# A two-layer encoder in fp32 on one core: 54 background columns with a scratch pool of their own, the rows' second column group for all tokens, and attention's first head with two depth pairs plain

## The chip, the cores and the metric

The kernel runs on one core of a Trainium2 chip. The metric is the device time of one execution in microseconds. Five engines matter: PE (matmul; its weight loads are listed as PEld), DVE (vector), ACT (scalar), POOL and SP. POOL and SP do little but issue DMAs here. All matrix products are fp32, made as three products of a high and a low half.

## The reference, cut to what matters

Batch 1, 512 tokens, width 2048, two layers, each with its own normalisation, conditioning, mixer and gate:

```python
mod = silu(c) @ ada_w                       # shifts, scales, gates: 128 columns of 128 numbers
# layer A: mLSTM, 8 heads, keys 256, values 512 wide
h = rmsnorm(x, g) * (1 + scale) + shift
qk = silu(causal_conv(h @ w_in[:, :4096]))  # 4 taps
v, o, z, gates = the rest of h @ w_in
ht = rmsnorm(mlstm(q, k, v, gates))         # per head: scores, decay, num / max(|den|, exp(-m))
x = x + gate * rmsnorm((sigmoid(o) * ht * silu(z)) @ a_w_out)
# one shared key and value from x
k, v = modulate(rmsnorm(x), ...) @ kv_w
# layer B: 16 heads, band of chunks, learned relative bias
q, z = modulate(rmsnorm(x), ...) @ b_w_in
x = x + gate * rmsnorm((attention(q, k, v) * silu(z)) @ b_w_out)
```

## The kernel before

Tokens stand along the free axis (512 columns), features on partitions. Weights come from one DRAM stream in **pieces** of 512 KB (128 x 1024 floats), in the order that `stream()` writes out, by SP's queue into three `raw` buffers. `split` makes two halves of each piece: the high one by a cast on ACT, the low one by a subtraction on DVE (both at line L243; tile `wh`). PE then runs `mm3` (L311): high·high, high·low, low·high. A piece serves 24 matmuls of 512 columns where all tokens go at once (2 depth tiles x 4 blocks, or 8 depth tiles of one block, x 3), and 12 where only one **token pair** of two goes (`PAIRS`).

Part of the products use half sums: `proj_s` and `proj_v` make seven products of 256 columns where eight would stand (banks D, C, A, B; sums of inputs by `three_sums`, sums of weights at L282 to L284, tiles `ws` and `wsh`). A product that does not use them is called **plain**. `proj_s` takes `f` depth pairs by half sums and the others plain; `pair_pieces` says which pairs share a piece.

The stages in time: an opening (0 to about 205 us) with the input's normalisation and the first products; mLSTM heads 0 and 1, plain (to about 430); head 2 (`HALF`) with a ramp, heads 3 to 7 by half sums (to about 1425); the product with `a_w_out`, here called **rows** (1425 to 1754), in four column groups `g` of 512: first depth half of all, then second depth half with group 0 for all tokens and groups 1 to 3 once per token pair; then residual, normalisation and transposes (`residual`, `turned`, `key_inputs`), values and keys (to 2076); 16 attention heads (to 2450); the last product and output.

**The background.** `mod` has one column of 128 numbers per 1 MB tile of `ada_w`: the tile `ada` is loaded and summed by one long DVE operation (L552, 2.3 us). Those needed early are made in the opening; 57 are made during heads 0 and 1 by calls of `background(n)`: sum up to n loaded tiles, then load until three are in flight, by POOL's queue. `SHIFTS` says how many of the 57 are shift columns of the second layer; the other shift columns (`whole`, 19) are loaded by SP and summed among the rows (`whole_steps`, `whole_sum`).

**Scratch.** Pool `tp`, tag `t`, has three buffers of 128 x 512. Convolution sums (`cv`), copies (`cu`, `g32`), squares (`sq`), gates (`sz`) and the two rows of each head (`row_out`: the norm's parts, written to DRAM by POOL's queue and read back into `f` by `factor`) all take turns in it.

**The order of the work.** The framework places each engine's instructions in a fixed order at build time from their data, their buffers and priorities; `tc.high_priority` moves an operation ahead, `pin` keeps operations in the program's order, `behind` puts one after another without a wait. What an engine waits for later does not change its order.

In attention, `queries(h, steps)` runs one head's `proj_s` over `b_w_in`; `steps` are calls between its pieces. The inputs `h2` and their sums `h2s` are made by `input_sums`, up to the first head's pieces.

## Time and profile before

| what | value |
|---|---|
| runs shown: median (lowest to highest) | 2637.78 us (2635.75 to 2638.52), 3 runs |
| the profiled execution | 2635.22 us |
| its span, mean granted clock of TensorE | 2633.4 us, 0.997 |
| PE, DVE, ACT busy | 2574.4, 2335.1, 1428.7 us |
| weight pieces of 512 KB by SP | 506 |
| DMA, HBM traffic over the span | 510.62 MB moved, 195 GB/s |

A row of waits reads: engine, operation and line, what it waited for, then the total in us, the count and the longest. A row of the timeline reads: start, length, engine, line, operation, tile written and tiles read, shapes, how many in a row, and in brackets the idle time before it with what ended it. A row of the windows gives the stretch, the busy time and number of instructions of PE, PEld, DVE, ACT and POOL, the granted clock of PE (1.00 is full), the busy share of the DMA engines and GB/s. "ps_..." are PSUM banks, "wh" and "wsh" split weights and weight sums.

### The profile page before, as it was taken

What the parts mean: (1) busy time and instruction counts of PE and PEld (TensorE: products, weight loads), DVE (VectorE), ACT (ScalarE), POOL (GpSimd) and SP (SyncE); (2) the same over time, 40 slices, a digit from 0 to 9 for tenths busy, and PEclk for the clock granted to TensorE, in tenths of its full rate; (3) what the DMA queues carried; (4) which work ended last, traced back from release to release, by engine and by line L of the source; (5) the groups of instructions that cost most, each with busy time, mean ns of one, the idle gap of its engine ahead of it and who ended that gap; (6) DMA issues with size and microseconds to landing.
All of it is one profiled execution on the core that took longest, in us unless ns stands there. A gap on an engine that the chain in (4) does not pass through costs nothing.

```text
span 2633.4 us, 45758 instructions
## 1 busy us (share of the span) xinstructions
PE 2574.4 (98%) x17994; PEld 2407.5 (91%) x17994; DVE 2335.1 (89%) x3812; ACT 1428.7 (54%) x2106; POOL 59.8 (2%) x118
## 2 busy tenths in 40 slices
PE   8999999999999999999999999999999999999998
PEld 6887787899999999999999898788999899999887
DVE  8978988999989999899998886977997999999767
ACT  4344533466555665556655453578543766776523
POOL 0000111000000000000000000000000000000000
PEclk9999999999999999999999999999999999999999
DMA  9876787533333333333336548988654544444787
GB/s 364 313 265 251 272 329 290 192 108 114 124 102 129 115 111 125 105 125 118 110 130 237 195 150 327 301 259 302 226 179 146 171 130 138 138 130 132 254 299 251
DMA packets 155315, 510.62 MB, mean 194 GB/s; under 512 B 17893, under 2 KB 31749, under 8 KB 140633
## 3 DMA queue, kind: packets, MB, share of 16 engines
q1 hardware_dynamic: 144346, 443.89, 49.6%
q0 software_dynamic: 10752, 63.79, 6.6%
q8 instruction: 141, 2.31, 0.4%
q14 instruction: 76, 0.62, 0.1%
HBM read 473.96 MB, written 38.90 MB: 195 GB/s over the span
## 4 chain that ended last, share of the span: by engine, by line
PE 56%; DVE 25%; DMA 8%; issue 7%; ACT 3%; POOL 0%; SPq 0%; DVEq 0%; ACTq 0%; POOLq 0%
DVE wh L243 6%; PE ps_y L311 5%; PE ps_azo L311 4%; PE ps_czo L311 4%; PE ps_dzo L311 4%; DVE ada L552 3%; PE ps_y_True L311 3%; PE ps_dz L311 3%; PE ps_cz L311 3%; PE ps_y_False L311 3%; PE ps_az L311 3%; DMA wr<-in_wst 3%; DVE wsh L243 2%; PE ps_bzo L311 2%; DVE cv L797 2%
## 5 line engine op out<-in xcount | busy, mean ns | idle before, releaser
L243 ACT CAST wh<-wr 128x1024 fp32r<-128x1024 f32 (+1 forms) x536 | 553.3, 1034 | 473.3 <-DVE wr L283 102.0
L243 DVE TENSOR_TENSOR wh<-wr,wh 128x1024 fp32r<-128x1024 f32 (+1 forms) x536 | 643.3, 1203 | 127.2 <-ACT wh L243 126.3
L243 ACT CAST wsh<-ws 128x768 fp32r<-128x768 f32 (+1 forms) x296 | 241.8, 817 | 298.4 <-PE ps_az L311 67.1
L243 DVE TENSOR_TENSOR wsh<-ws,wsh 128x768 fp32r<-128x768 f32 (+1 forms) x296 | 276.8, 935 | 45.7 <-ACT wsh L243 44.5
L552 DVE CUSTOM_DVE_ANT_0 ada<-ada,scB,cl 128x2048 f32<-128x2048 f32 (+1 forms) x89 | 205.8, 2322 | 11.3 <-DMA ada<-in_adaT 11.2
L282 DVE TENSOR_TENSOR ws<-wr 128x512 f32<-128x512 f32 (+1 forms) x296 | 198.5, 673 | 5.3 <-DMA wr<-in_wst 5.0
L311 PE MATMUL ps_y_False<-wh,y 128*128 128x512 f32 x768 | 168.6, 380 | 2.3 <-DVE wh L243 2.2
L311 PE MATMUL ps_y<-wh,y 128*128 128x512 f32 x768 | 168.6, 380 | 0.1
L311 PEld LDWEIGHTS ps_y_False<-wh,y 128*128 128x128 f32 x768 | 144.3, 189 | 24.4 <-DVE wh L243 4.2
L311 PEld LDWEIGHTS ps_y<-wh,y 128*128 128x128 f32 x768 | 144.3, 189 | 20.8 <-DVE wh L243 0.5
L311 PE MATMUL ps_kv<-wh,hkv 128*128 128x512 f32 x576 | 127.3, 381 | 1.6 <-DVE wh L243 1.5
L311 PE MATMUL ps_v<-wh,h 128*128 128x512 f32 x576 | 127.3, 380 | 0.0
L311 PEld LDWEIGHTS ps_kv<-wh,hkv 128*128 128x128 f32 x576 | 108.0, 189 | 18.5 <-DVE wh L243 3.3
L284 DVE TENSOR_TENSOR ws<-wr 128x256 f32<-128x256 f32 (+1 forms) x296 | 122.1, 414 | 3.1
L283 DVE TENSOR_TENSOR wr<-ws,wr 128x256 f32<-128x256 f32 (+1 forms) x296 | 121.8, 413 | 2.4
L311 PEld LDWEIGHTS ps_v<-wh,h 128*128 128x128 f32 x576 | 108.3, 189 | 15.8 <-issue 0.9
L311 PE MATMUL ps_l<-h,wh 128*128 128x512 f32 x480 | 107.7, 380 | 2.1 <-DVE wh L243 2.1
L311 PEld LDWEIGHTS ps_l<-h,wh 128*128 128x128 f32 x480 | 90.3, 189 | 16.5 <-DVE wh L243 3.3
L311 PE MATMUL ps_azo<-h,wh 128*128 128x256 f32 (+1 forms) x606 | 92.9, 285 | 0.0
L311 PE MATMUL ps_y_True<-wh,y 128*128 128x512 f32 x384 | 83.3, 379 | 0.0
L311 PEld LDWEIGHTS ps_y_True<-wh,y 128*128 128x128 f32 x384 | 72.5, 189 | 10.2
L311 PEld LDWEIGHTS ps_azo<-h,wh 128*128 128x128 f32 x606 | 79.2, 192 | 1.1
(431 smaller groups left out, 5825.2 us busy)
## 6 DMA issues: line engine op xcount, KB each, us to landing
wr<-in_wst SPq DMA_DIRECT2D x506, 512.0 KB, 3.7
ada<-in_adaT POOLq DMA_DIRECT2D x57, 1024.0 KB, 7.1
ada<-in_adaT SPq DMA_DIRECT2D x49, 1024.0 KB, 7.0
ada<-in_adaT SPq DMA_DIRECT2D x36, 512.0 KB, 6.5
wr<-in_wst SPq DMA_DIRECT2D x26, 384.0 KB, 6.2
xt<-nsc SPq DMA_DIRECT2D x32, 256.0 KB, 3.8
yr<-ysc SPq DMA_DIRECT2D x28, 256.0 KB, 5.4
ysc<-zo SPq DMA_DIRECT2D x24, 256.0 KB, 3.9
```

The lines of the kernel that those rows point to most:

```text
L243: ins = nc.scalar.copy(hi, src), nc.vector.tensor_tensor(lo, src, hi.bitcast(F32), op=ALU.subtract)
L282: nc.vector.tensor_tensor(t[:, : 2 * w], r[:, w : 3 * w], r[:, : 2 * w], op=ALU.subtract)
L283: nc.vector.tensor_tensor(r[:, w : 2 * w], t[:, w : 2 * w], r[:, :w], op=ALU.add)
L284: nc.vector.tensor_tensor(t[:, 2 * w :], r[:, 3 * w :], r[:, w : 2 * w], op=ALU.subtract)
L311: product[0] = nc.tensor.matmul(ps, a, b, start=start, stop=stop)
L552: pin(nc.vector.tensor_tensor_reduce(c, c, (sc or scB)[:, j * w : (j + 1) * w], 1.0, mod[:, i : i + 1] if j else col(CB + i), ALU.mult, AL ...
L797: nc.vector.scalar_tensor_tensor(acc[:, d:], ps[:, : S - d], col(CW + 32 * (3 - d) + ch), acc[:, d:], op0=ALU.mult, op1=ALU.add)
```

## The change

It has four parts. Lines of the changed kernel stand some rows further down: L311 is L316 there, L243 is L248, L552 is L560.

1. **Background.** `SHIFTS` goes from 9 to 6: 54 columns in the front, and 22 instead of 19 among the rows. Four tiles may be in flight, in a ring over two pools' buffers and one of a new pool. The calls begin six steps earlier in the opening, and from then on are spread: one sum between the two pieces of a block (`mid`) and smaller counts elsewhere.
2. **A pool `t0`** from the end of the opening, with three buffers for convolution sums, two for copies, two for rows and one for an ada tile; it serves heads 0 to 2 (rows: 0 and 1), which leave `tp`. Head 0's mask sum stands after its v product, and the loads of the relative bias move from all heads to heads 3 to 7.
3. **Rows.** Group 1 runs for all tokens (8 pieces) with seven column loads between its pieces; only groups 2 and 3 run per token pair. This takes 8 pieces out of the stream. The calls of three groups of the second pair stand in two; some key inputs and transposes move on into the values; the last token group's `xr` goes into the key sums' buffers.
4. **Attention's first head.** `ATT_FIRST` is 6: pairs 6 and 7 are plain in head 0. Its first two pieces are half-sum pieces of two pairs each, the others one half-sum pair and one plain pair (`late`); a plain product into bank B is done as two halves of 256. The sums of pairs 6 and 7 (`plain_sums`) are made at steps 2 and 3 of head 0.

In counts: PE has 12 more matmuls of 512 columns and 18 fewer of 256; SP issues 8 transfers of 512 KB fewer and 3 of 1 MB more, POOL 3 of 1 MB fewer; ACT and DVE have 8 splits of a piece fewer each.

```diff
@@ -30 +30 @@
-SHIFTS = 9
+SHIFTS = 6
@@ -48,0 +49 @@
+ATT_FIRST = 6
@@ -81 +82 @@
-def pair_pieces(f, merged=False):
+def pair_pieces(f, merged=False, late=False):
@@ -87,0 +89,3 @@
+    if late:
+        out = [([[a]], [b]) for a, b in zip(sk[f - n :], nk)]
+        return [([sk[i : i + 2]], []) for i in range(0, f - n, 2)] + out
@@ -119,2 +123,2 @@
-    def tile_s(mat, c1, c2, f, merged=False):
-        for sk, nk in pair_pieces(f, merged):
+    def tile_s(mat, c1, c2, f, merged=False, late=False):
+        for sk, nk in pair_pieces(f, merged, late):
@@ -155,0 +160 @@
+    tile_b("a_w_out", 512, KT)
@@ -157 +162 @@
-        for g in range(1, 4):
+        for g in range(2, 4):
@@ -167 +172 @@
-        tile_s("b_w_in", h * P, D + h * P, ATT_PAIRS, True)
+        tile_s("b_w_in", h * P, D + h * P, ATT_PAIRS if h else ATT_FIRST, True, True)
@@ -322 +327 @@
-    def proj(mat, xs, pss, nk, k0, k1, last, t0=0, t1=S, first=None):
+    def proj(mat, xs, pss, nk, k0, k1, last, t0=0, t1=S, first=None, mid=None):
@@ -325,0 +331,2 @@
+            if mid and ka > k0:
+                mid()
@@ -333,2 +340,2 @@
-    def proj_a(mat, xs, ps, t0=0, t1=S):
-        proj(mat, xs, [ps], 8, 0, len(xs), len(xs) - 1, t0, t1)
+    def proj_a(mat, xs, ps, mid):
+        proj(mat, xs, [ps], 8, 0, len(xs), len(xs) - 1, mid=mid)
@@ -358 +365 @@
-    def proj_s(mat, xs, ss, f, z1, z2, name, pl, bufs, at={}, merged=False, banks="pppp", lead=AHEAD):
+    def proj_s(mat, xs, ss, f, z1, z2, name, pl, bufs, at={}, merged=False, banks="pppp", lead=AHEAD, late=False):
@@ -363 +370 @@
-        pieces = pair_pieces(f, merged)
+        pieces = pair_pieces(f, merged, late)
@@ -382 +389,2 @@
-                            acc(ps, slice(0, S), main, b0 + 4 * m + 2 * j + t, xs[2 * k + j], False)
+                            for w in (h0, h1_) if late and t else (slice(0, S),):
+                                acc(ps, w, main, b0 + 4 * m + 2 * j + t, xs[2 * k + j][:, :, w], False)
@@ -676 +684 @@
-    loaded = []
+    loaded, ring = [], [(ap_, 2), (ap_, 2), (bp, 1)]
@@ -688,2 +696,3 @@
-        while pending and len(loaded) < 3:
-            p, bufs = (bp, 1) if len(pending) % 3 == 1 else (ap_, 2)
+        while pending and len(loaded) < len(ring):
+            p, bufs = ring.pop(0)
+            ring.append((p, bufs))
@@ -694 +703 @@
-        if n > len(steps) - 6:
+        if n > len(steps) - 12:
@@ -733,0 +743,2 @@
+    ep = mst.enter_context(pool("t0", side="right"))
+    ring.insert(0, (ep, 1))
@@ -752 +763 @@
-        g32 = tp.tile([P, S], F32, tag="t", name="g32")
+        g32 = early_tile(True, "cu", 2, "g32")
@@ -787 +798,2 @@
-    def conv(ps, ch, name, lead, woven):
+    def early_tile(h, tag, bufs, name):
+        return ep.tile([P, S], F32, tag=tag, name=name, bufs=bufs) if h else tp.tile([P, S], F32, tag="t", name=name)
@@ -789 +801,3 @@
-        acc = tp.tile([P, S], F32, tag="t", name=f"cv_{name}")
+    def conv(ps, ch, name, lead, woven, early):
+
+        acc = early_tile(early, "cv", 3, f"cv_{name}")
@@ -792 +806 @@
-                rows = tp.tile([P, S], F32, tag="t", name=f"cu_{name}")
+                rows = early_tile(True, "cu", 2, f"cu_{name}")
@@ -885 +899 @@
-        r = tp.tile([P, S], F32, tag="t", name=f"row{h}_{i}")[0:1]
+        r = early_tile(h < HALF, "row", 2, f"row{h}_{i}")[0:1]
@@ -935,2 +949,2 @@
-                proj_a("a_w_in", h1, ps)
-            qk.append(conv(ps, chs[i], f"{h}_{i}", AHEAD if h == HALF else 100 if h > HALF and i > 1 else 0, h in (0, HALF)))
+                proj_a("a_w_in", h1, ps, lambda: background(1))
+            qk.append(conv(ps, chs[i], f"{h}_{i}", AHEAD if h == HALF else 100 if h > HALF and i > 1 else 0, h in (0, HALF), h <= HALF))
@@ -938 +952 @@
-                background(2)
+                background(1)
@@ -949 +963 @@
-            background(2)
+            background(1)
@@ -956,3 +970,8 @@
-        nc.vector.tensor_tensor(
-            nmd, nm.rearrange("p (a b) -> p a b", a=4), maskd.unsqueeze(1).to_broadcast([P, 4, P]), op=ALU.add
-        )
+
+        def masked():
+            nc.vector.tensor_tensor(
+                nmd, nm.rearrange("p (a b) -> p a b", a=4), maskd.unsqueeze(1).to_broadcast([P, 4, P]), op=ALU.add
+            )
+
+        if h:
+            masked()
@@ -962 +981 @@
-            add_at(at, {k: lambda: background(2) for k in (0, 4, 8)})
+            add_at(at, {k: lambda: background(1) for k in (4, 12)})
@@ -964 +983 @@
-            for k in range(0, KT, 2):
+            for k in (0, 2, 4, 8, 12):
@@ -981 +1000 @@
-        for i in (2 * h, 2 * h + 1):
+        for i in range(BH * (h - HALF - 1) // (NH - HALF - 1), BH * (h - HALF) // (NH - HALF - 1)) if h > HALF else ():
@@ -983,0 +1003 @@
+            masked()
@@ -1000 +1020 @@
-            background(2 + (h == 0))
+            background(1)
@@ -1013 +1033 @@
-                proj_a("a_w_in", h1, ps)
+                proj_a("a_w_in", h1, ps, lambda: background(1))
@@ -1022 +1042 @@
-                proj_a("a_w_in", h1, ps)
+                proj_a("a_w_in", h1, ps, lambda: background(1))
@@ -1030,2 +1049,0 @@
-        if h == 0:
-            background(2)
@@ -1070 +1088 @@
-            background(3)
+            background(1 + h)
@@ -1178 +1196 @@
-    xrs = [[] for _ in range(4)]
+    xrs, fetched_xr = [[] for _ in range(4)], [0] * 4
@@ -1182,2 +1200,7 @@
-        for g in range(len(xrs[m]), len(xrs[m]) + n):
-            xrs[m].append(xr_p.tile([P, S], F32, tag="xr", name=f"xr{m}_{g}"))
+        for g in range(fetched_xr[m], fetched_xr[m] + n):
+            if m < 3:
+                xrs[m].append(xr_p.tile([P, S], F32, tag="xr", name=f"xr{m}_{g}"))
+            else:
+                if g % 2 == 0:
+                    t = kp.tile([P, 2, S], F32, tag="k", name=f"xr{m}_{g}", bufs=KT)
+                    xrs[m] += [t[:, i, :] for i in range(2)]
@@ -1184,0 +1208 @@
+        fetched_xr[m] += n
@@ -1315,0 +1340,2 @@
+    gate_row(0, 1)
+    rows(1, range(4), ys, whole_steps(3, (0, 2, 4, 6, 8, 10, 12)))
@@ -1317,2 +1343 @@
-        for g in range(1, 4):
-            at = {}
+        for g in range(2, 4):
@@ -1320 +1345 @@
-                at = whole_steps(3, (0, 6, 12)) if g < 3 else whole_steps(3, (0,)) | {k: whole_sum for k in (4, 8, 12)}
+                at = whole_steps(3, (0, 6, 12)) if g < 3 else {k: whole_sum for k in (0, 4, 8)}
@@ -1324 +1349 @@
-            if pair == 1 and g == 1:
+            elif g == 2:
@@ -1327 +1352 @@
-            if pair == 1 and g == 2:
+            else:
@@ -1329,2 +1354 @@
-            if pair == 1 and g == 3:
-                at = {k: lambda k=k: key_inputs(1 + k // 2 % 2) for k in range(2, KT, 2)}
+                add_at(at, {k: lambda k=k: key_inputs(1 + (k in (6, 12))) for k in range(2, KT, 2)})
@@ -1356 +1380 @@
-    hs, h2, h2s, fetched = [], [], [], []
+    hs, h2, h2s, fetched, plain = [], [], [], [], {}
@@ -1383 +1407 @@
-                    w = slice(0, 256 + 256 * i)
+                    w = slice(0, S if k >= ATT_FIRST else 256 + 256 * i)
@@ -1384,0 +1409,4 @@
+                if k >= ATT_FIRST:
+                    plain[k] = raw
+                    h2s.append(None)
+                    continue
@@ -1394 +1422 @@
-            turn = {2 + 6 * i: lambda i=i: turned(1, [i], True) for i in range(3)} if pair == 0 and g == 1 else {}
+            turn = {k: lambda i=i: turned(1, [i], True) for i, k in enumerate((4, 8, 14))} if pair == 0 and g == 1 else {}
@@ -1436 +1463,0 @@
-    tst.close()
@@ -1460 +1487 @@
-        proj_s("b_w_in", h2, h2s, ATT_PAIRS, z1, z2, f"z{h}", kq, (2, 2), steps, True)
+        proj_s("b_w_in", h2, h2s, ATT_PAIRS if h else ATT_FIRST, z1, z2, f"z{h}", kq, (2, 2), steps, True, late=True)
@@ -1527,0 +1555,3 @@
+    def plain_sums(k):
+        h2s[k] = three_sums(plain[k], kq, f"h2s{k}", ATT_PAIRS, h2[2 * k][:, :, 256:], True)
+
@@ -1552 +1582,9 @@
-            qs[h], szs[h] = queries(h, {1: turn, 2: mid, 3: end})
+            steps = {1: turn, 2: mid, 3: end}
+            if h == 0:
+                add_at(steps, {2 + i: lambda k=k: plain_sums(k) for i, k in enumerate(plain)})
+            qs[h], szs[h] = queries(h, steps)
+            if h == 0:
+                for k, raw in plain.items():
+                    s1 = h2s[k][0]
+                    split(s1[:, 0, :], s1[:, 1, :], raw[0][:, 256:])
+                tst.close()
```

DVE at the end of head 0 (`oz` are head 0's gated outputs, `sqs` the sum of its squares, `f` the rows read back from DRAM, `sp_q` the split that PE's `ps_q` reads). Before:

```order
L1054 TENSOR_TENSOR oz_1_258<-ps_n_1_2022,oz_1_258 128x512
L1054 TENSOR_TENSOR oz_2_259<-ps_n_2_2037,oz_2_259 128x512
L1057 TENSOR_TENSOR sqs_2008<-sqs_2008,sq_1_2033 128x512
L1057 TENSOR_TENSOR sqs_2008<-sqs_2008,sq_2_2048 128x512
L1054 TENSOR_TENSOR oz_3_260<-ps_n_3_2052,oz_3_260 128x512
L1057 TENSOR_TENSOR sqs_2008<-sqs_2008,sq_3_2063 128x512
L243 TENSOR_TENSOR sp_q_2068<-sqs_2008,sp_q_2068 128x512
L956 TENSOR_TENSOR nmd_2126<-nm_2125,maskd 128x512
L552 ISA ada_0_1979,mod<-ada_0_1979,scB,cl 128x2048
L552 ISA mod 128x1
L243 TENSOR_TENSOR wh_2390<-wr_2388,wh_2390 128x1024
L552 ISA ada_0_1995,mod<-ada_0_1995,scB,cl 128x2048
```

Now:

```order
L1072 TENSOR_TENSOR oz_0_257<-ps_n_0_2003,oz_0_257 128x512
L1072 TENSOR_TENSOR oz_1_258<-ps_n_1_2016,oz_1_258 128x512
L1075 TENSOR_TENSOR sqs_2002<-sqs_2002,sq_1_2027 128x512
L1072 TENSOR_TENSOR oz_2_259<-ps_n_2_2031,oz_2_259 128x512
L1075 TENSOR_TENSOR sqs_2002<-sqs_2002,sq_2_2042 128x512
L911 TENSOR_TENSOR f_2070<-f_2070 16x32
L1072 TENSOR_TENSOR oz_3_260<-ps_n_3_2046,oz_3_260 128x512
L1075 TENSOR_TENSOR sqs_2002<-sqs_2002,sq_3_2057 128x512
L560 ISA ada_0_1979,mod<-ada_0_1979,scB,cl 128x2048
L560 ISA mod 128x1
L248 TENSOR_TENSOR wh_2281<-wr_2279,wh_2281 128x1024
L248 TENSOR_TENSOR sp_q_2062<-sqs_2002,sp_q_2062 128x512
```

The first operation on `f`, which stood in head 1 behind its `cv` and `qk`, now stands among the sums of squares, ahead of `sp_q`.

PE at the scores of head 1 (`ps_s`, from the convolved `qk`). Before, among the o products:

```order
L311 MATMUL ps_s_0_2272<-qk_0_2095,qk_2_2113 128x512 x2
L311 MATMUL ps_s_1_2326<-qk_0_2095,qk_2_2113 128x384 x2
L311 MATMUL ps_s_2_2373<-qk_0_2095,qk_2_2113 128x256 x2
L311 MATMUL ps_o_0_2480<-h_1_302,wh_2483 128x512 x3
L311 MATMUL ps_s_0_2272<-qk_0_2095,qk_2_2113 128x512
L311 MATMUL ps_s_1_2326<-qk_0_2095,qk_2_2113 128x384
L311 MATMUL ps_s_2_2373<-qk_0_2095,qk_2_2113 128x256
L311 MATMUL ps_o_0_2480<-h_2_393,wh_2483 128x512 x3
```

Now, among the v products:

```order
L316 MATMUL ps_s_0_2257<-qk_0_2083,qk_2_2101 128x512 x2
L316 MATMUL ps_v_0_2117<-wh_2281,h_8_765 128x512 x3
L316 MATMUL ps_v_1_2118<-wh_2281,h_8_765 128x512 x3
L316 MATMUL ps_v_2_2119<-wh_2281,h_8_765 128x512 x3
L316 MATMUL ps_v_3_2120<-wh_2281,h_8_765 128x512 x3
L316 MATMUL ps_v_0_2117<-wh_2281,h_9_833 128x512 x3
L316 MATMUL ps_s_0_2257<-qk_0_2083,qk_2_2101 128x512
L316 MATMUL ps_v_1_2118<-wh_2281,h_9_833 128x512 x3
```

The scores come earlier by most of a v product, so their inputs are needed earlier.

PE at the third piece of attention's head 0 (`h2s` are the sums of inputs, `h` the plain inputs). Before:

```order
L311 MATMUL ps_dz_21816<-h2s_42_21637,wh_21936 128x256 x3
L311 MATMUL ps_dz_21816<-h2s_42_21690,wh_21936 128x256 x3
L311 MATMUL ps_dz_21816<-h_8_21622,wh_21936 128x256 x3
L311 MATMUL ps_dz_21816<-h_10_21675,wh_21936 128x256 x3
L311 MATMUL ps_cz_21817<-h2s_3_21634,wsh_0_21939 128x256 x3
L311 MATMUL ps_cz_21817<-h2s_3_21687,wsh_0_21939 128x256 x3
```

Now:

```order
L316 MATMUL ps_az_21754<-h_12_21689,wh_21882 128x512 x3
L316 MATMUL ps_bz_21755<-h_12_21689,wh_21882 128x256 x6
L316 MATMUL ps_az_21754<-h_13_21692,wh_21882 128x512 x3
L316 MATMUL ps_bz_21755<-h_13_21692,wh_21882 128x256 x6
L316 MATMUL ps_dz_21752<-h2s_42_21598,wh_21882 128x256 x3
L316 MATMUL ps_dz_21752<-h_8_21583,wh_21882 128x256 x3
L316 MATMUL ps_cz_21753<-h2s_3_21595,wsh_0_21885 128x256 x3
L316 MATMUL ps_cz_21753<-h_8_21583,wsh_0_21885 128x256 x3
```

The piece began with two pairs of sums; it begins with a plain pair and has one pair of sums.

## The prediction

> **What bounds the kernel now.** I read the page first, then the waits of PE by stretch, then PE's timeline at the longest of them, then the windows around these places for the granted clock and the DMA rate.
>
> ```profile
> span 2633.4 us, 45758 instructions
> PE 2574.4 (98%) x17994; PEld 2407.5 (91%) x17994; DVE 2335.1 (89%) x3812; ACT 1428.7 (54%) x2106; POOL 59.8 (2%) x118
> PE 56%; DVE 25%; DMA 8%; issue 7%; ACT 3%; POOL 0%; SPq 0%; DVEq 0%; ACTq 0%; POOLq 0%
> ```
>
> PE is busy for 2574.4 of 2633.4 us: whatever else is done, 59 us of idle time and the time under a lowered clock are all that a change can win without taking matmuls away. The chain passes through DVE for a quarter of the span: in most stretches PE is bound, and in a few it waits for a split on DVE. So I list PE's waits in the three stretches that the change touches: the plain heads (170 to 480 us), the rows with the start of the keys (1590 to 1860), and the start of attention (2030 to 2110).
>
> ```profile
> PE ps_s L311 <- ACT qk L243: 4.4, 1, 4.4
> PE ps_q L311 <- ACT sp_q L243: 3.8, 1, 3.8
> PE ps_z L311 <- DVE wh L243: 3.4, 2, 2.7
> PE ps_n L311 <- DVE so L1054: 1.3, 1, 1.3
> PE ps_at L782 <- DVE ssum L773: 1.2, 1, 1.2
> PE ps_d L311 <- ACT sp_d L243: 0.5, 1, 0.5
> PE ps_n L311 <- ACT row L886: 0.5, 1, 0.5
> PE ps_li L311 <- ACT g L753: 0.2, 1, 0.2
> ...
> PE ps_y_False L311 <- DVE wh L243: 2.2, 4, 0.8
> PE ps_x L1220 <- DVE xn L1212: 1.9, 1, 1.9
> PE ps_kv L311 <- DVE wh L243: 1.5, 3, 0.8
> ...
> PE ps_dz L311 <- DVE h2s L243: 1.8, 1, 1.8
> PE ps_dz L311 <- ACT h2s L243: 1.7, 1, 1.7
> ```
>
> The columns after the colon are the total, the count and the longest, in us. The plain heads hold 15.3 us in eight kinds of wait, the rows and keys 5.6 in these three, the start of attention 3.5.
>
> Waiting is not all that such a place costs. Here is what the clock did after three of them (PE's timeline, then the windows, whose last three columns are granted clock, DMA share and GB/s):
>
> ```profile
> 315.09 2.21 PE L311 MATMUL ps_s<-qk,qk 128*128 128x512 f32 x6 [4.37 <-ACT qk L243]
> 422.90 0.48 PE L311 MATMUL ps_q<-sp_q,ones_r 128*128 128x512 f32 x1 [3.81 <-ACT sp_q L243]
> 2086.34 0.83 PE L311 MATMUL ps_dz<-h,wh 128*128 128x256 f32 x6
> 2092.53 0.38 PE L311 MATMUL ps_dz<-h2s,wh 128*128 128x256 f32 x1 [1.68 <-ACT h2s L243]
> 2094.68 0.79 PE L311 MATMUL ps_dz<-h2s,wh 128*128 128x256 f32 x2 [1.77 <-DVE h2s L243]
> 2096.55 1.49 PE L311 MATMUL ps_cz<-h2s,wsh 128*128 128x256 f32 x6
> ...
> 312.00:316.00 4.00, 0.91 (x2) 0.76 (x3) 4.00 (x5) 3.40 (x6) 0.26 (x1) 0.90 0.49 187
> 316.00:320.00 4.00, 4.00 (x16) 3.56 (x15) 4.00 (x7) 3.95 (x5) 0.27 (x1) 0.67 0.69 248
> 350.00:400.00 50.00, 47.32 (x220) 41.11 (x219) 43.07 (x40) 13.42 (x15) 7.44 (x14) 1.00 0.99 391
> 400.00:450.00 50.00, 43.70 (x211) 37.62 (x210) 41.48 (x49) 17.10 (x24) 7.26 (x14) 1.00 0.78 300
> 1350.00:1400.00 50.00, 50.00 (x450) 50.00 (x450) 47.33 (x79) 31.28 (x37) 0.00 (x0) 1.00 0.37 124
> 1450.00:1500.00 50.00, 50.00 (x233) 43.80 (x232) 47.74 (x77) 22.73 (x38) 0.00 (x0) 1.00 0.61 212
> 2090.00:2094.00 4.00, 1.24 (x9) 0.85 (x7) 3.69 (x8) 3.22 (x5) 0.00 (x0) 0.94 0.40 155
> 2094.00:2098.00 4.00, 3.32 (x15) 3.32 (x16) 4.00 (x8) 1.42 (x2) 0.00 (x0) 0.50 0.41 131
> 2098.00:2106.00 8.00, 8.00 (x64) 8.00 (x63) 7.19 (x15) 4.67 (x7) 0.00 (x0) 0.85 0.27 86
> ```
>
> After the gap of 4.37 us the mean clock was 0.90 and then 0.67: 4 × 0.10 + 4 × 0.33 = 1.7 us lost. After the gap of 3.81 the window shows 1.00. At the start of attention two gaps of 1.68 and 1.77 lie around a lone matmul, and six matmuls then take 1.49 us instead of 0.83: 4 × 0.06 + 4 × 0.50 + 8 × 0.15 = 3.4 us lost. Two full windows give PE's rates: 50 / 233 = 214.6 ns for a matmul of 512 columns, 50 / 450 = 111 ns for one of 256.
>
> **The front (plain heads 0 and 1).** What the change removes here are waits that come from shared buffers (the last row is the page's on the column sums' tiles on POOL's queue: count, KB, us to landing):
>
> ```profile
> 378.90 2.35 DVE L552 CUSTOM_DVE_ANT_0 ada<-ada,scB,cl 128x2048 f32<-128x2048 f32 x1 [2.16 <-DMA ada<-in_adaT]
> 385.01 1.05 ACT L243 CAST wh<-wr 128x1024 fp32r<-128x1024 f32 x1 [4.91 <-DMA wr<-in_wst]
> 420.22 0.60 ACT L1053 ACTIVATE sq<-ps_n 128x512 f32<-128x512 f32 x1 [5.69 <-DMA dsc<-row]
> 420.64 0.48 POOL L893 DMA_DIRECT2D f<-dsc  x1 [7.78 <-DMA dsc<-row]
> 427.09 0.49 POOL L893 DMA_DIRECT2D f<-dsc  x1 [1.52 <-DMA dsc<-row]
> ...
> ada<-in_adaT POOLq DMA_DIRECT2D x57, 1024.0 KB, 7.1
> ```
>
> *ps_z, 3.4.* DVE waited for an ada tile and ACT for a weight piece at the same time: the DMA engines were the limit, 391 GB/s at a share of 0.99. In the order of DVE 18 column sums stand before the 12 pieces wh64 to wh75 (25.2 MB of both kinds); a piece of 24 matmuls takes 24 × 0.2146 = 5.15 us, so 12 ask for 25.2 MB in 61.8 us, 407 GB/s, over the ceiling. Now 22 sums stand before the 16 pieces wh60 to wh75: 31.5 MB in 82.4 us, 382 GB/s, just under it, with four tiles in flight instead of three. I leave 0.7.
>
> *ps_q, 3.8.* ACT's square waited 5.69 us for a scratch buffer that a row's small transfer held, which took 7.78 us behind ada tiles on POOL's queue. Rows have buffers of their own now. But the order of DVE has moved the first operation of f (which waits for row to DRAM and back, both on POOL's queue) from far behind head 0 to between its squares' sums, and the last sums, sp_q, one ada sum and a weight split are queued behind it. Lower bound: two transfers as at 427.09, 0.49 + 1.52 us each, begun at ps_d while three ps_n groups run: nothing. Upper bound: both behind ada tiles, R1 below. I take 2: in POOL's order one tile load stands ahead of the row, begun about 5 us earlier by my count of what lies between (four short DVE products, a weight split of 1.2 us, the split sp_d, ps_d and the row on ACT), so of its 7.1 us some 2 are left.
>
> *ps_s, 4.4 and 1.7 of clock.* The convolutions' tiles came from the same three scratch buffers; they have three and two of their own. The scores of head 1 also move from the o products forward into its v products, so qk must be ready earlier. I leave 1.5 between nothing and the old 4.4, and no lowered clock.
>
> *The rest, 3.7.* Gates and the ends of the two heads keep their chains, with fewer sums in them: 1.7 stay, and 0.5 more for the earlier beginning of the sums near 160 to 200 us (R3). Together 0.7 + 2 + 1.5 + 1.7 + 0.5 = 6.4 stay of 17.0: **−10.6**, between −15 and −2. Three column sums fewer run here (57 loads to 54 on POOL's queue); DVE is not what ends PE's waits where they stood, so their 3 × 2.35 us count for nothing by themselves, and the three that go to the rows take places of pieces there.
>
> **Rows and keys.** Eight pieces are no longer fetched and split twice: eight transfers of 0.524 MB, eight casts (1.05 us, the row at 385.01) and eight DVE splits. Three 1 MB tiles come in, so the traffic falls by 4.2 − 3.1 = 1.1 MB, and PE's matmuls are the same. The cover is in the second group: 24 matmuls per piece instead of 12. Behind it the work stays (two token pairs by two groups), so what pair 1 had in three groups (residual, transposes, key inputs, loads of x) now stands in two of 41 us: the waits of ps_y_False can go, the transposes' 1.9 stays since each still follows its residual in the same stretch, and ACT is closer to full. From 2.2 + 1.5 of removable waits against new ones of that size where three groups' side work stands in two I take **−1**, between −3 and +3.
>
> **Start of attention.** Head 0's third piece holds the two gaps: PE came to pairs 4 to 7 with the sums of the last pairs not yet split. Two of eight depth pairs become plain there, their sums are made while head 0 runs, and the third piece begins with plain products that need only split inputs. The price: +12 matmuls of 512 and −18 of 256 columns by the order, 12 × 0.2146 − 18 × 0.111 = 0.6 us. The gain: 3.45 of gaps and 3.4 of clock. The deferred sums come later on DVE, beside the splits for head 1, which at worst makes PE wait about 1.1 us (a DVE piece split of 1.22, the length of one that would stand ahead) for the bank of head 1; I take half. 3.45 + 3.4 − 0.6 − 0.55: **−5.7**, between −6.3 and −4.
>
> The Trainium skill ("TensorE: Matmul & The Clock Gate", "What's actually happening") says that the clock is halved after an idle window of about 3.4 us, on a free-running window. By that rule read as one gap, neither 1.68 nor 1.77 would have cost clock, this part would be worth 2.3 and the sum −13.9; the trace shows the loss after the pair of them, and none after 3.81, so the rows are kept.
>
> **Sum.** −10.6 − 1 − 5.7 = −17.3. The profiled execution took 2635.2 us (span 2633.4), the median of the runs is 2637.8, 2.6 longer; the difference is taken from the median: 2620.5, so **2620**.
>
> **Rivals.**
>
> *R1, the early f blocks DVE* (0.14). If the row's transfers go behind ada tiles, one takes 7.8 us as at 420.64, DVE stands about 6 us before the squares' last sum, and PE's ps_q with it, long enough for 1.7 of clock as after 4.37: 7.7 instead of 2. For: before, both transfers were on the same queue with the tiles. Against: then two tiles were issued in the microseconds ahead of the row, now one. 2620.5 + 5.7 = 2626.
>
> *R2, the DMA ceiling still binds* (0.14). 382 of 391 GB/s leaves 2%; scattered small transfers can eat that. Then ps_z keeps 3.4, head 1's scores keep about 4, and the rows, where DMA's share rises in pair 1, gain nothing: 2.7 + 2.5 + 1 back plus 1.7 of clock: 2620.5 + 7.9 = 2628.
>
> *R3, late tiles at the earlier start* (0.09), the slower one. The background now begins at wh33, in six more calls of the opening loop.
>
> ```profile
> DMA to landing us min/median/max: 5.0/7.0/14.2
> 150.00:200.00 50.00, 50.00 (x233) 43.80 (x232) 37.99 (x47) 26.05 (x33) 2.65 (x5) 1.00 0.63 224
> ```
>
> Two tiles per two steps of 18 matmuls (3.87 us each) leave 7.7 us for a landing of 7.1; DVE, with 12 us of 50 free, would stall on a late one and the weight splits with it. If six calls were each 4 us late (the longest landing would make it 14.2 − 7.7 = 6.5): 24 + 1.7 of clock, 2620.5 + 25.7 = 2646. It decides from a landing of about 7.7 + (17.3 + 5.3) / 6 = 11.5 us, within the longest seen, 14.2. Against: the share is 0.63 there.
>
> *R4, all goes* (0.09): −15 − 3 − 6.3: 2613.
>
> *R5, the front does not do what it says* (0.06): each wait taken out there comes back one operation later, as the chain is the same; only attention's part holds: 2632.
>
> **How the numbers follow.** The forecast has 0.48. Its own range is 2614 to 2625, from half of each part's bounds. From R4's side to R5's, with some room for waits that no view names: **2608 to 2633**, which leaves out R3 and tails, under 2 in 10. What a measurement of this kernel can tell from no change is about 0.2%, 5.3 us. Faster: the forecast, R1, R2 and R4 with a third of R5, less tails: 0.83. Same: most of R5 and tails: 0.08. Slower: R3: 0.09.
>
> **What would show it.** Right, step by step: in the plain heads PE's waits sum to about 6 and no window there is below 1.00 in clock; the square on ACT waits for no row transfer; windows at 2090 to 2106 stand at 1.00 with no ps_dz gap of h2s; ps_y_False waits less than 1 us; ps_x still near 1.9. Wrong: a gap at ps_q or sp_q behind f (R1); DVE waiting for ada with DMA at 0.99 in head 1 (R2); lost time before 200 us (R3); new waits in pair 1 of the rows or at the first key products above 5 us, which no case holds.

## The result, and the profile after

The changed kernel takes 2618.2 us (median of 6 runs, 2617.1 to 2622.3) against 2637.5 for the kernel before on the same chip: a ratio of 0.9928, 95% interval 0.9914 to 0.9942. That is about 19 us less, between 15 and 23 by the interval. The forecast was 2620. The profiled execution's span is 2616.7 us, 16.7 less than the 2633.4 before. Its page:

```profile
span 2616.7 us, 45705 instructions
PE 2570.2 (98%) x17988; PEld 2404.6 (92%) x17988; DVE 2324.7 (89%) x3804; ACT 1418.5 (54%) x2096; POOL 57.9 (2%) x115
...
ada<-in_adaT POOLq DMA_DIRECT2D x54, 1024.0 KB, 8.6
```

PE and DVE have about as much work as before (4.2 and 10.4 us less busy); what went is idle time and time at a lowered clock. A tile of a column sum now takes 8.6 us to land at the median, not 7.1; four may be under way instead of three.

PE's waits in the three stretches that were listed before (plain heads; rows and keys; start of attention):

```profile
PE ps_li L316 <- ACT g L764: 2.3, 1, 2.3
PE ps_at L793 <- DVE ssum L784: 1.4, 1, 1.4
PE ps_l L316 <- ACT oz L966: 0.3, 1, 0.3
PE ps_s L316 <- DVE qk L248: 0.2, 1, 0.2
...
PE ps_x L1244 <- DVE hkv L248: 2.8, 2, 2.4
PE ps_x L1244 <- DVE xn L1236: 1.4, 2, 0.7
PE ps_kv L316 <- DVE wh L248: 1.0, 3, 0.6
PE ps_y_False L316 <- DVE wh L248: 0.8, 2, 0.5
...
PE ps_cz L316 <- DVE z L420: 2.8, 1, 2.8
```

In the plain heads 4.2 us are left of 15.3; of the four long waits (ps_s, ps_q, ps_z, ps_n) 0.2 us at ps_s are left. In the rows and keys 6.0 stand where 6.1 stood, on other operations. At the start of attention both ps_dz gaps are gone and one of 2.8 us at ps_cz, in head 1, has come.

The two windows that mattered most, the second half of head 1 (columns as before: granted clock, DMA share, GB/s at the end) and the start of attention's heads 1 and 2:

```profile
350.00:400.00 50.00, 50.00 (x233) 43.78 (x232) 45.24 (x40) 13.03 (x15) 7.40 (x14) 1.00 0.99 399
...
2080.00:2110.00 30.00, 27.18 (x237) 26.76 (x236) 29.44 (x62) 20.60 (x33) 0.00 (x0) 1.00 0.38 123
```

PE is full in the first (47.3 of 50 before), with the DMA engines at the same share and 399 GB/s. In the second, DVE is busy for 29.4 of 30 us.

To see where the time went I compare the starts of the same products in both timelines. The table gives, for a profiled execution of each kernel, how much earlier (−) than in the kernel before the first v product of head 3, the first one by half sums, starts (**front**; so head 2 is in it), what the stretch from the rows' second depth half to the start of attention's head 0 takes more or less (**rows and keys**), and the same for attention up to the last product's start (**attention**). "Again" is the changed kernel profiled a second time. The other rows are the experiments below. One run of "again" (2919.8 us at a granted clock of 0.851) and one of "all three undone" (7734.1 us) stand far outside the others and are left out of the medians.

| kernel | front | rows and keys | attention | median of runs | ratio to before, 95% interval |
|---|---|---|---|---|---|
| changed | −14.6 | −0.3 | −2.0 | 2618.2 | 0.9928 (0.9914 to 0.9942) |
| again | −15.6 | +1.4 | −1.8 | 2616.9 | 0.9917 (0.9897 to 0.9936) |
| attention undone | −13.6 | +2.5 | −2.1 | 2619.3 | 0.9926 (0.9912 to 0.9941) |
| scratch undone | −13.9 | +0.0 | −1.9 | 2621.1 | 0.9933 (0.9918 to 0.9948) |
| calls and fourth tile undone | −9.0 | −0.6 | −2.2 | 2624.1 | 0.9945 (0.9928 to 0.9961) |
| all three undone | +3.3 | +2.0 | −3.5 | 2636.3 | 0.9998 (0.9985 to 1.0011) |
| scratch and fourth tile undone | +0.9 | −1.6 | −2.1 | 2628.0 | 0.9966 (0.9954 to 0.9977) |
| old rows, 54 columns in front | −12.8 | +8.5 | −2.8 | 2625.5 | 0.9948 (0.9933 to 0.9963) |
| old rows, 57 in front | −16.8 | −1.2 | −4.4 | 2619.3 | 0.9928 (0.9911 to 0.9946) |
| new rows, 57 in front | −14.6 | −0.2 | −1.2 | 2619.4 | 0.9932 (0.9912 to 0.9952) |
| head 0's banks | −16.0 | −0.1 | −4.2 | 2619.1 | 0.9922 (0.9906 to 0.9938) |
| old rows, 57, banks | −13.9 | −0.9 | −2.4 | 2618.9 | 0.9927 (0.9912 to 0.9941) |
| new rows, 57, banks | −16.1 | +2.5 | −3.3 | 2621.2 | 0.9941 (0.9926 to 0.9956) |

So most of the gain is the front's. A cell is one execution: where two kernels have the same instructions in a stretch, they still differ by 1 to 3 us there, and only larger differences, or ratios whose intervals lie apart, are read as effects. An interval reaches some 4 us to either side, so the difference of two kernels is known to about 5 us.

### The profile page after: what moved, and what is told of

It is laid out like the page before. It is cut to its first block, busy times and chain, and to the rows that moved or that the text cites. A ratio compares the mean times of both kernels' runs of the same rounds, so it can differ in the third digit from the quotient of the medians.

```text
span 2616.7 us, 45705 instructions
## 1 busy us (share of the span) xinstructions
PE 2570.2 (98%) x17988; PEld 2404.6 (92%) x17988; DVE 2324.7 (89%) x3804; ACT 1418.5 (54%) x2096; POOL 57.9 (2%) x115
## 5 line engine op out<-in xcount | busy, mean ns | idle before, releaser
L248 ACT CAST wh<-wr 128x1024 fp32r<-128x1024 f32 (+1 forms) x528 | 544.9, 1034 | 483.9 <-DVE wr L288 104.3
L248 DVE TENSOR_TENSOR wh<-wr,wh 128x1024 fp32r<-128x1024 f32 (+1 forms) x528 | 636.3, 1208 | 134.4 <-ACT wh L248 133.5
L248 ACT CAST wsh<-ws 128x768 fp32r<-128x768 f32 (+1 forms) x296 | 241.3, 815 | 294.9 <-PE ps_az L316 60.9
L248 DVE TENSOR_TENSOR wsh<-ws,wsh 128x768 fp32r<-128x768 f32 (+1 forms) x296 | 277.6, 938 | 44.8 <-ACT wsh L248 43.7
L560 DVE CUSTOM_DVE_ANT_0 ada<-ada,scB,cl 128x2048 f32<-128x2048 f32 (+1 forms) x86 | 199.0, 2323 | 3.6 <-DMA ada<-in_adaT 3.3
L316 PE MATMUL ps_y<-wh,y 128*128 128x512 f32 x768 | 168.6, 380 | 0.0
L316 PE MATMUL ps_y_False<-wh,y 128*128 128x512 f32 x768 | 167.7, 380 | 0.8 <-DVE wh L248 0.8
L316 PEld LDWEIGHTS ps_y_False<-wh,y 128*128 128x128 f32 x768 | 144.5, 189 | 21.8 <-DVE wh L248 1.6
L316 PEld LDWEIGHTS ps_y<-wh,y 128*128 128x128 f32 x768 | 144.3, 189 | 20.7 <-DVE wh L248 0.4
L316 PE MATMUL ps_kv<-wh,hkv 128*128 128x512 f32 x576 | 128.5, 384 | 1.1 <-DVE wh L248 1.0
L316 PE MATMUL ps_v<-wh,h 128*128 128x512 f32 x576 | 127.6, 380 | 0.0
L316 PEld LDWEIGHTS ps_kv<-wh,hkv 128*128 128x128 f32 x576 | 109.0, 191 | 18.2 <-DVE wh L248 2.9
L316 PEld LDWEIGHTS ps_v<-wh,h 128*128 128x128 f32 x576 | 108.2, 189 | 15.8 <-issue 0.9
L316 PE MATMUL ps_l<-h,wh 128*128 128x512 f32 x480 | 108.4, 381 | 3.0 <-DVE wh L248 2.1
L316 PEld LDWEIGHTS ps_l<-h,wh 128*128 128x128 f32 x480 | 90.0, 189 | 18.6 <-DVE wh L248 3.5
L316 PE MATMUL ps_azo<-h,wh 128*128 128x256 f32 (+1 forms) x606 | 92.9, 285 | 0.0
L316 PE MATMUL ps_y_True<-wh,y 128*128 128x512 f32 x384 | 83.3, 379 | 0.0
L316 PEld LDWEIGHTS ps_y_True<-wh,y 128*128 128x128 f32 x384 | 72.5, 189 | 10.2
L316 PEld LDWEIGHTS ps_azo<-h,wh 128*128 128x128 f32 x606 | 79.3, 192 | 1.1
```

Of the source, the lines that this page charges most:

```text
L248: ins = nc.scalar.copy(hi, src), nc.vector.tensor_tensor(lo, src, hi.bitcast(F32), op=ALU.subtract)
L316: product[0] = nc.tensor.matmul(ps, a, b, start=start, stop=stop)
L560: pin(nc.vector.tensor_tensor_reduce(c, c, (sc or scB)[:, j * w : (j + 1) * w], 1.0, mod[:, i : i + 1] if j else col(CB + i), ALU.mult, AL ...
```

## The experiments

**The same kernel again.** No edit.

> The changed kernel once more, unchanged, to see how far one profiled execution of the same instructions differs from another, stage by stage. Run with attention's part undone, whose order is the same as the changed kernel's up to the last inputs of attention, stood 1.0 us elsewhere at the end of the front and 2.2 us elsewhere at the end of the keys. If that is scatter, this run will differ from the first by as much: 2616 to 2621. If it is an effect of the undone part, this run repeats the first within 0.3 us at each place: 2618.

Measured: 2616.9. Of the second execution the front came out 1.1 us shorter, rows and keys 1.7 longer. So one execution differs from another of the same instructions by such amounts, and the kernel with attention undone, whose instructions are the same up to the last inputs of attention, lies within that up to there. Attention's stage repeated within 0.2 here, but over all nine kernels and executions that run the changed attention with the old banks it lies anywhere from −1.2 to −4.4 (mean −2.4).

**Attention undone.**

```diff
-ATT_FIRST = 6
+ATT_FIRST = 8
```

> Only attention's first head goes back to eight pairs by half sums; the other parts of the change stay. As predicted, the part is worth 5.7 us, and this would take 2618.2 + 5.7 = 2624. By what the profile of the changed kernel shows at this place (head 1 starts 5.8 us earlier after the start of head 0, but PE then waits 2.8 us at ps_cz for the eviction of head 0's bank, and a steady head later only 2.0 us are left), it is worth 2.0: 2620, the gap and the half clock at head 0's third piece are back, and the wait at ps_cz is gone.

Measured: 2619.3, and 2.1 us gained in attention against the kernel before, though its code there is the old one. PE's timeline at head 0's third piece, and the window behind it:

```profile
2080.49 0.38 PE L316 MATMUL ps_dz<-h2s,wh 128*128 128x256 f32 x1 [0.68 <-ACT h2s L248]
2082.64 0.49 PE L316 MATMUL ps_dz<-h2s,wh 128*128 128x256 f32 x2 [1.77 <-DVE h2s L248]
...
2083.00:2087.00 4.00, 4.00 (x24) 4.00 (x23) 4.00 (x7) 1.42 (x2) 0.00 (x0) 0.57 0.24 94
```

The gaps are back, but the first is 0.68 and not 1.68, and the half clock lasts for 4 × 0.43 = 1.7 us and not 3.4. So 2.7 us of what the prediction took as this stage's loss were absent in an execution in which the same instructions arrived a little earlier; whether the changed stages ahead or scatter brought them earlier isn't told apart. The plain pairs were worth nothing measurable (2619.3 against 2618.2 and 2616.9, the intervals nearly the same). The 5.7 falls.

**Banks for head 0.** What the plain pairs gained before head 1 they lost in it: in the changed kernel head 1 starts 19.6 us after head 0, in the kernel before 25.4, and then come the 2.8 us at ps_cz, where PE needs the bank that DVE has not yet evicted. This run takes that wait alone away:

```diff
-        proj_s("b_w_in", h2, h2s, ..., steps, True, late=True)
+        proj_s("b_w_in", h2, h2s, ..., steps, True, banks="pppp" if h else "aapa", late=True)
```

> Attention's head 0 takes its banks D, C and B from the other PSUM pool, so that head 1's first piece finds free banks and PE needn't wait for the eviction of head 0; nothing else changes, and DVE's order is the same. Theory W (the 2.8 us at ps_cz are a wait for a bank and nothing else): the wait goes and a steady head is 2.8 us earlier against the start of head 0: 4.8 instead of 2.0, 2615.5. Theory V (DVE is full from the start of the third piece on, and PE has run ahead of it): most of it comes back as waits for weight sums wsh or weights wh in the next two pieces, 1 us or less is left: 2617.5.

Measured: 2619.1, and in the stage −4.2 instead of −2.0 and −1.8. The wait at ps_cz is gone, and a steady head is 2.3 us earlier in this execution, which is nearer to theory W; in the two later kernels with these banks the stage stood at −2.4 and −3.3. The mean of the three, −3.3, is 0.9 more than the −2.4 without them, and both groups overlap. New waits behind DVE come in (PE's timeline of this run, then its window):

```profile
2101.08 1.09 PE L1529 MATMUL ps_t<-kcs,s 128*128 128x128 f32 x6 [0.80 <-DVE s L1520]
2112.95 0.48 PE L316 MATMUL ps_s<-k,q 128*128 128x512 f32 x1 [0.41 <-DVE q L248]
...
2078.00:2108.00 30.00, 29.20 (x256) 28.72 (x255) 29.45 (x63) 21.66 (x35) 0.00 (x0) 1.00 0.37 123
```

DVE is busy for 29.45 of 30 us, as it was. In the two later kernels the wait at ps_t is 1.9 and 1.7 us. So most of the wait came back behind DVE in two of three executions: theory V's reason, though at ps_t and not at the weights where it had put it. About 1 us is left by the mean, which the medians don't tell from nothing.

**The front: scratch.** Three things change there: where the background's calls stand, a fourth tile in flight, and scratch tiles of their own. First the scratch undone:

```diff
     def early_tile(h, tag, bufs, name):
-        return ep.tile([P, S], F32, tag=tag, name=name, bufs=bufs) if h else tp.tile([P, S], F32, tag="t", name=name)
+        return tp.tile([P, S], F32, tag="t", name=name)
```

> The new pool keeps only its ada tile; the convolution sums, copies and rows take the three shared scratch buffers again; the background's calls, the rows and attention stay as changed. Theory S (the front's waits came from the shared scratch): ps_s, ps_q and the clock come back, about 4.4 + 3.8 + 1.7 = 10 us, 2628. Theory B (they came from the background's sums and tiles, crowded into too few places): at most 2 us come back, 2620.

Measured: 2621.1, the front 0.7 and 1.7 us longer than in the two executions with the pool. Theory S falls in the main: neither ps_q's wait nor the lowered clock came back. The waits of PE in its plain heads:

```profile
PE ps_s L316 <- DVE e L881: 2.4, 1, 2.4
PE ps_s L316 <- ACT qk L248: 1.1, 2, 0.8
PE ps_li L316 <- ACT g L764: 0.9, 1, 0.9
PE ps_at L793 <- DVE ssum L784: 0.9, 1, 0.9
```

At ps_s 3.5 us stand again (0.2 with the pool, 4.4 before); the front is hardly longer since the gates' waits, ps_li and ps_at, are 1.9 shorter.

**The front: calls and the fourth tile.** The scratch pool stays, the rest goes back.

```diff
-        if n > len(steps) - 12:
+        if n > len(steps) - 6:
...
-    ring.insert(0, (ep, 1))
...
-                proj_a("a_w_in", h1, ps, lambda: background(1))
+                proj_a("a_w_in", h1, ps, None)
...
-            add_at(at, {k: lambda: background(1) for k in (4, 12)})
+            add_at(at, {k: lambda: background(2) for k in (0, 4, 8)})
...
```

> The background's calls go back to their old places and counts, with three tiles in flight (54 columns still), and the new pool serves the scratch tiles as changed. Theory S: only the weight waits at ps_z (3.4) come back, and the 2 us that the opening and the gates had lost are regained: about 2620. Theory B: most of the front's gain is lost, about 10 us: 2628.

Measured: 2624.1, the front −9.0 instead of −14.6 and −15.6. Between the theories: ps_z has its wait again (3.0 us), ps_s has 1.4 of its 4.4 and ps_q nothing; the granted clock is 0.97 in two windows of 50 us, 3.0 us more. Undoing either half lost only a part of the gain, so I undid both.

**The front: all three.** The two edits above together.

> Both halves of the front's change undone together: old calls, three tiles in flight, and scratch tiles from the three shared buffers; 54 columns, rows and attention as changed. Undoing the scratch alone cost 0.6 us at the end of head 1, undoing the calls alone 5.8. If the two replace each other (each alone takes away the wait at the scores that both would): the front's whole gain of 14.5 is lost, but for the three columns (3 x 2.35 us of DVE, at most 2 us here): 2631. If they add up: 6.4 us are lost, 2624.5.

Measured: 2636.3, a ratio of 0.9998: the whole gain of the kernel is gone. Its longest waits in the plain heads are again ps_z, ps_s, ps_n and ps_q:

```profile
PE ps_z L316 <- DVE wh L248: 3.8, 3, 2.4
PE ps_s L316 <- ACT qk L248: 3.2, 1, 3.2
PE ps_n L316 <- DVE so L1073: 2.2, 1, 2.2
PE ps_q L316 <- ACT sp_q L248: 1.8, 1, 1.8
```

So the halves replace each other in part. Undoing the scratch costs about 3.6 us and undoing calls and tile 6.6 (medians against 2617.5, the mean of 2618.2 and 2616.9), both together 18.8; the 3.6 alone is not told from nothing. The front says the same: 1.2 and 6.1 us longer alone (against the mean, −15.1), 18.4 together. The place is seen best at ps_q. The first two rows are from the run with the scratch alone undone, the last from this one, each at the end of head 1:

```profile
408.29 0.60 ACT L1071 ACTIVATE sq<-ps_n 128x512 f32<-128x512 f32 x1 [1.19 <-PE ps_n L316]
412.22 0.49 POOL L907 DMA_DIRECT2D f<-dsc  x1 [8.46 <-DMA dsc<-row]
...
421.77 0.60 ACT L1072 ACTIVATE sq<-ps_n 128x512 f32<-128x512 f32 x1 [5.30 <-DMA dsc<-row]
```

With the scratch alone undone the row's transfer is as slow as before (POOL waited 8.46 us for it), but no square on ACT waits for it; with both undone a square does, for 5.30 us. Three columns fewer, the rows and the attention part, which this kernel still has, gave together nothing that the interval (3 to 4 us either way) shows.

**The front: only the calls.**

```diff
-    ring.insert(0, (ep, 1))
...
-        return ep.tile([P, S], F32, tag=tag, name=name, bufs=bufs) if h else tp.tile([P, S], F32, tag="t", name=name)
+        return tp.tile([P, S], F32, tag="t", name=name)
```

> Of the front's change only the places and counts of the background's calls are left: scratch tiles from the three shared buffers, three tiles in flight; the new pool stays empty. If spreading the calls alone does it: front as without the scratch pool, 13.9 us less than before, 2621. If the fourth tile in flight was what carried it, the waits for weights (ps_z, ps_s, ps_q) come back and half of the gain goes: 2628.

Measured: 2628.0. By medians, from all undone: the calls' places bring 8.3 us, the fourth tile on top 6.9, the scratch on top of both 3.6. The first two are clear of their 5 us, the last is not. (The profiled execution of this kernel was the slowest of its ten, 7 us above the median; its +0.9 in the table is that execution's.) PE's waits in its plain heads did not come back where they were expected: 4.4 us at ps_n and 2.6 at ps_li, but 1.0 at ps_s, 0.4 at ps_z and nothing at ps_q. The fourth tile was not undone alone, with the pool in place, nor kept alone with the old calls. What it does shows in the groups of instructions between 150 and 430 us: the row of the column sums, with DVE's idle time before them at its end. First the changed kernel, then the one without the scratch pool, then the one with only the calls:

```profile
L560 DVE CUSTOM_DVE_ANT_0 ada<-ada,scB,cl 128x2048 f32<-128x2048 f32 x50 | 116.6, 2346 | 2.7 <-DMA ada<-in_adaT 2.5
```

```profile
L560 DVE CUSTOM_DVE_ANT_0 ada<-ada,scB,cl 128x2048 f32<-128x2048 f32 x50 | 116.5, 2343 | 1.3 <-DMA ada<-in_adaT 1.3
```

```profile
L560 DVE CUSTOM_DVE_ANT_0 ada<-ada,scB,cl 128x2048 f32<-128x2048 f32 x48 | 112.3, 2345 | 12.7 <-DMA ada<-in_adaT 12.5
```

With three tiles DVE waits 12.5 us for them here, and 10.9, 10.9 and 13.7 in the kernel before and the two runs with the old calls; in all ten kernels and executions with four tiles it waits 1.3 to 3.6. The wait stands in DVE's queue ahead of weight splits, convolutions and squares, and so can reach PE as a wait for any of them; no run shows which of PE's waits it made.

**Rows: the old second group.** The group per token pair again, its transposes and loads of x as before, with the new stream's 22 columns.

```diff
-    rows(1, range(4), ys, whole_steps(3, (0, 2, 4, 6, 8, 10, 12)))
...
-        for g in range(2, 4):
+        for g in range(1, 4):
...
+                at = whole_steps(3, (0, 4, 8, 12)) if g < 3 else whole_steps(3, (0, 4)) | {k: whole_sum for k in (8, 10, 12)}
...
```

> The rows' second column group runs per token pair again, with its three groups of calls in the second pair as before (and 15 column loads among them, three more than before). As predicted the part is worth 1 us: 2619. By the profile, in which the rows and keys took 0.3 us less than before: 2618.5. If the eight pieces are what makes the later stages' room, a loss of 3 or more: 2621.

Measured: 2625.5, and 8.5 us more than before in rows and keys. Its waits there, and the windows around the longest two:

```profile
PE ps_y_False L315 <- DVE wh L247: 5.3, 4, 2.8
PE ps_y_False L315 <- ACT wh L247: 1.8, 1, 1.8
PE ps_x L1237 <- DVE rsn L1190: 1.7, 1, 1.7
...
1635.00:1660.00 25.00, 20.40 (x88) 16.79 (x87) 19.76 (x20) 9.55 (x12) 0.00 (x0) 0.94 0.84 301
1660.00:1685.00 25.00, 25.00 (x109) 21.57 (x108) 17.45 (x16) 9.44 (x9) 0.00 (x0) 0.93 0.81 297
```

The first token pair's pieces come late (4.6 us in two waits), and 25 × 0.06 + 25 × 0.07 = 3.3 us go to the clock.

**Old rows, 57 columns in front.** This asks whether the old group or the three columns in it cost that.

```diff
-SHIFTS = 6
+SHIFTS = 9
...
-            background(1 + h)
+            background(1 + 4 * h)
```

and the rows' loops of the kernel before.

> 57 columns in the front, the three more summed at the end of head 1, and the rows exactly as before (second group per token pair, 19 columns); new calls, pool and attention as changed. Against the run with the old rows and 22 columns, which lost 8.5 us between the start of the second half of the rows and the key products. Theory M (the three columns moved are what that cost, and the new group pays for them): the rows take again what they took before, 0 instead of 8.5, and the front loses at most 2 for the three columns: 2619 to 2621. Theory P (my places for the calls cost it, or the new front shifts the rows' loads): the loss stays above 5: 2624.

Measured: 2619.3, with rows and keys at −1.2: theory M. The old group has no room for three columns more, at least not at the places that I gave them; other places weren't tried.

**New rows, 57 in front.** The fourth corner.

```diff
-SHIFTS = 6
+SHIFTS = 9
...
-    rows(1, range(4), ys, whole_steps(3, (0, 2, 4, 6, 8, 10, 12)))
+    rows(1, range(4), ys, whole_steps(3, (0, 4, 8, 12)))
```

> 57 columns in the front (the three more at the end of head 1) and the rows' second group for all tokens with four column loads in it instead of seven; calls, pool and attention as changed. This completes a square: old rows took 1.2 us less than before from the second depth half to the last value products with 19 columns and 8.5 us more with 22, the new rows with 22 about the same as before (0.3 less and 1.4 more in two executions). If columns cost wherever they are put (theory M), the new rows without the three gain some 3 us or more: 2615. If the new rows have room for them, nothing: 2618.

Measured: 2619.4, rows and keys −0.2: the new group has room for the three columns, and without them it has no gain of its own. Three corners of the square have 2617.5, 2619.3 and 2619.4, and only old rows with 22 columns stand apart. The new group pays for the columns moved into it, and the front, which they left, had no use for the room (−14.6 and −16.8 with 57, −14.6 and −15.6 with 54).

**A version that beats both?** The banks with 57 columns, on old rows and on new.

> The best of the parts seen so far with the old rows: new calls and pool, 57 columns, rows as before, attention's first head with plain pairs and with banks for head 0 from the other pool. The old rows with 57 columns had 2619.3 and a profiled span of 2613.4; the banks gave 2.3 us more than the changed kernel in the stage. If the parts add up: 2615 to 2617. If the runs' scatter hides it: 2619.

> As the run with the old rows and the banks, with the new rows and 57 columns. If the new rows gain without the three columns: 2613; if not, as the other: 2616 to 2619.

Measured: 2618.9 and 2621.2. Neither is told from the changed kernel; of what was tried nothing beats it.

## Why the prediction was right, and where it was not

The sum, −17.3, stood: −16.7 in the profiled execution, −19 by the ratio. Its terms did not. The front was worth 14.6 and 15.6 instead of 10.6, rows and keys between −0.3 and +1.4 instead of −1, attention 2.0 and 1.8 instead of 5.7 (and as much, 2.1, with the part undone). Two misses of about 4 us went against each other: that the sum came out so close is luck.

*The front's waits.* The prediction named the right waits and left 6.4 us of them; 4.2 stayed. Too much was left at ps_q (2; nothing stayed), ps_s (1.5; 0.2) and ps_z (0.7; nothing). Too little was left at the gates and head ends, 1.7 with 0.5 for the opening; there 4.0 are left, 2.3 at ps_li, 1.4 at ps_at and 0.3 at ps_l. Not in the sum at all were 2.0 us in head 2 (0.73 at ps_bzo and 1.27 at a ps_n in the timeline before), of which 0.8 are left.

*ps_q and the early f.* The prediction ran two places together: the wait of 3.8 us stood at the end of head 1, the early f stands at the end of head 0. There the row had landed 2.0 us after POOL had issued its transfer. POOL's timeline in the changed kernel (the last row is at the end of head 1):

```profile
274.57 0.50 POOL L901 DMA_DIRECT2D dsc<-row  x1 [4.45 <-ACT row L900]
277.03 0.49 POOL L907 DMA_DIRECT2D f<-dsc  x1 [1.97 <-DMA dsc<-row]
...
286.55 0.48 POOL L901 DMA_DIRECT2D dsc<-row  x1 [9.03 <-ACT row L900]
...
411.74 0.49 POOL L907 DMA_DIRECT2D f<-dsc  x1 [9.05 <-DMA dsc<-row]
```

In head 0 f's first operation ran at 279.3 on DVE without a wait, and the second transfer stands behind the sums of squares and holds nobody. In head 1 a row took the 9 us that R1 feared, but there f comes behind sp_q in DVE's order, and the row has a buffer that no square needs. The lower bound was the right one, and R1 did not occur.

*The cause given for ps_s and ps_q.* The prediction put them down to shared scratch alone and ps_z to a DMA ceiling. With the scratch shared again, ps_q's wait and the lowered clock stayed away and 3.5 us at ps_s came back. So for ps_q sharing is needed but not enough: the old calls with three tiles must come with it. That they act by making DVE late (11 to 14 us of waiting for tiles) fits the rows but was not shown by itself. The step "what the change removes here are waits that come from shared buffers" is half of it: the releaser that the profile names is the last of two.

*The ceiling.* 391 GB/s at a share of 0.99 was taken for the most that the DMA engines give, and the gain at ps_z was worked out from 407 asked against 382. In that window the four kernels with three tiles moved 379 to 391 GB/s and the ten executions with four 389 to 409 (399 in the changed kernel), at shares of 0.97 to 1.01. So 391 was not the most; whether 409 is near it, no run shows. With four tiles 1.3 to 3.6 us of DVE's 11 to 14 of waiting were left, at a rate only a few per cent higher. ps_z has no wait left: R2 did not occur.

*Rows and keys, −1.* The size is within the scatter. But the step was right for another reason than given: "the three that go to the rows take places of pieces there" hid two terms, +8.5 for three columns in the old group and as much back from the new one. One sign failed: ps_x, forecast near 1.9, has 4.2, and one of its gaps cost 1.7 us of clock (*The clock*, below).

*Attention, −5.7.* "At worst PE waits about 1.1 us" for head 1's bank is the step that failed: it was 2.8 and 2.3 in the two executions, and in the second a lowered clock took 1.7 more. DVE was full for the 30 us after, and not just behind one weight split. And the 3.4 us of clock were a price of one execution: with the part undone the same place had 1.7.

*R3* came in small: the opening and the gates have 2.3 and 1.4 us of waits that were 0.2 and 1.2, far from 24. The tiles landed in 8.6 us at the median, 13.0 at most, and the sums still waited 2.5 us in all.

*The clock.* The prediction set the Trainium skill's rule ("TensorE: Matmul & The Clock Gate", "What's actually happening") against the rows of before. The changed kernel's rows bear out that the length of one gap does not decide. Here are two gaps of it, with the windows around them, and at the end the gap at ps_cz in its second execution:

```profile
1773.25 0.95 PE L1244 MATMUL ps_x<-kcs,xn 128*128 128x128 f32 x4 [2.44 <-DVE hkv L248]
2085.39 0.94 PE L316 MATMUL ps_cz<-h2s,wsh 128*128 128x256 f32 x6 [2.82 <-DVE z L420]
...
1772.00:1776.00 4.00, 2.75 (x9) 2.37 (x10) 3.54 (x6) 4.00 (x10) 0.00 (x0) 0.68 0.85 299
1776.00:1780.00 4.00, 4.00 (x18) 3.39 (x18) 1.46 (x4) 2.18 (x5) 0.00 (x0) 0.89 0.81 231
2082.00:2086.00 4.00, 1.18 (x11) 0.99 (x10) 4.00 (x9) 2.40 (x5) 0.00 (x0) 1.00 0.63 230
2086.00:2090.00 4.00, 4.00 (x35) 3.85 (x35) 3.97 (x7) 1.73 (x4) 0.00 (x0) 1.00 0.04 16
...
2085.41 0.94 PE L316 MATMUL ps_cz<-h2s,wsh 128*128 128x256 f32 x6 [2.29 <-DVE z L420]
2084.00:2088.00 4.00, 2.59 (x17) 2.50 (x18) 3.96 (x10) 1.04 (x1) 0.00 (x0) 0.86 0.33 131
2088.00:2092.00 4.00, 4.00 (x28) 4.00 (x28) 3.83 (x7) 3.57 (x5) 0.00 (x0) 0.71 0.23 78
```

A gap of 2.44 us between short transposes lost 4 × 0.32 + 4 × 0.11 = 1.7 us of clock. At ps_cz one of 2.82 lost none, as 3.81 had lost none before, and in the second execution one of 2.29 lost 4 × 0.14 + 4 × 0.29 = 1.7. The Trainium skill ("TensorE: Matmul & The Clock Gate", "What's actually happening") calls the window free-running, so where it falls could explain why 2.82 lost nothing; but the losses after 2.44 and 2.29 came below its 3.4 us, and no run here tests either.

## What to carry to other kernels

Where several waits fall away together, undo each cause alone and then all of them: two causes that replace each other look small one by one (3.6 and 6.6 us) and are worth 18.8 together. Before the rate of a background stream that an in-order engine sums is called a limit, try one more tile in flight: here it took some 11 us of waiting from DVE (12.5 to 1.3 with the scratch shared) while the rate in the fullest window rose from 381 to 405 GB/s. Before a gap of PE is priced as a gain, look at the engine behind it: if that is full for the next stretch, most of the gap may only move.
